# A decoder step's sparse-attention indexer: the new tokens' scores in one step at the head of the chain, with more slack for every index product

## The chip, the cores and the metric

The kernel runs on one core of a Trainium2 chip. The metric is the device time of one execution in microseconds, the median of several runs; lower is better. The core has a matrix engine (PE, with its weight loads shown as PEld), a vector engine (DVE), an activation engine (ACT), a general engine (POOL) and a queue engine (SP) that issues most transfers.

## The reference, cut to what matters

One inference step of one decoder layer: 256 prompt tokens and 64 sample tokens (8 requests of 8 new tokens, each with 2048 cached positions in 16 pages) go through one input projection whose columns feed three head groups; their outputs are gated, joined and go through one output projection and a layer norm. The change touches the indexer of the sample tokens. For each request it scores all 2056 keys, the 2048 cached ones and the 8 new ones, and the top 256 of each query are attended to:

```python
def _indexer_scores(iq, iw, ik):
    dots = jnp.einsum('bthd,bld->bthl', iq.astype(jnp.float32), ik.astype(jnp.float32)) * (D_IDX ** -0.5)
    return jnp.einsum('bth,bthl->btl', iw.astype(jnp.float32) * (H_IDX ** -0.5), jax.nn.relu(dots))
# in _dsa_sample
ik_all = jnp.concatenate([ik_past.astype(ik_new.dtype), ik_new], axis=1)
sc = _indexer_scores(iq, iw, ik_all)
sc = jnp.where(kpos[None, None, :] <= qpos[None, :, None], sc, -jnp.inf)
_, sel = lax.top_k(sc, n_sel)
```

There are 16 index heads of width 64, so a request's 8 queries times 16 heads fill the 128 rows of a product.

## The kernel before, in words

**Data.** Products that need more than one pass of precision are done on split numbers: `ACT.copy` rounds a tile to a short float (`wh` of a weight half `wr`, `xh` of the input), the difference is kept (`wl`, `xl`), and three products stand for one: high by high, low by high, high by low. A weight block of 128 columns by 8 slices of 128 rows comes by one transfer into `wr`; each half of it (512 columns) becomes a pair `wh`, `wl`, ACT making the first and DVE or POOL the second. A half serves 12 products `pj<-x..,w..`, in two quanta of six. There are four buffers each of `wh` and `wl`.

**Order of the work.** One program order is written out by a planner while the kernel is built. `Plan` keeps a reckoned time for each engine and each tile; the main loop at the end of `hymba_step` puts the next piece on PE: a quantum of six projection products, a unit of two cache pages (`KV` or `VACC` products on tiles of 32 columns), or a step of one of the background generators (`bg`). A generator yields `need(tiles, ps=.., lag=..)`, and is taken up again (`met`) when all the tiles are available by the plan for at least `lag` us and `ps` of the buffers `mA`, `mB` in the matrix engine's accumulator memory are free. So a lag is a distance in reckoned time between the operands and the product that reads them: projection quanta are put in between. Once recorded, each engine executes its list in order, and waits where an operand or a buffer is late on the chip.

**The index chain of the sample tokens** is the generator `idx_sample`. It waits for the eight index-query blocks (`iq`), which `ev_iq` adds into the tile `st["q"]` on DVE, and splits that tile: `ACT.copy(qh, q)` and `DVE.tensor_sub(ql, q, qh)`. Then it walks through steps. A step (`stack`) takes 512 keys of each of two requests, stacks high and low parts of the keys above each other (two `ACT.copy` of 64 rows, two `DVE.tensor_sub` of 64 rows), and does four products of 512 columns, two for each request. A relu of each result goes to SBUF on ACT or DVE. After four such pairs of steps `sums` weighs the relus by head and adds them (products on tiles of 32 columns into `va`). Requests come in two halves `sp`; each half had the cached keys in four step pairs and, as the part `c == 2`, the 8 new keys of its four requests in two more steps of four products of 8 columns, with their own sums. That made 20 steps. The cached index keys are gathered by `idx_load` through POOL and SP.

Beside it run `idx_prompt` (index scores of the prompt tokens: blocks of products with 64 rows, into all four `mA`, `mB` buffers, evacuated by ACT into `PT`), and later `topk_sample`, `soft`, the cache pages, `hgrn`, `attn_*`, the memory products and the output projection, which all take their place from the same planner. `LAG2` is the lag of a step's products behind their operands.

Of the kernel before, what the change touches and what calls it, by code (L numbers as in the profile page):

```python
# [38 lines left out]
PATIENCE = 9.0  # L39
SOON = 0.4  # L40
LAG = 1.5
LAG2 = 0.4
VISIT_WAIT = 9.0
HASTE = 2.0
CALM = 4.0
# [175 lines left out]
def need(*aps, ps=1, lag=0.0, visit=0.0):  # L221

    return (aps, ps, lag, visit)
# [3 lines left out]
def hymba_step(ctx: ExitStack, tc: tile.TileContext, I, O):  # L227
# [673 lines left out]
    def idx_sample():  # L901
# [10 lines left out]
        qlr = ql.rearrange("p b h t -> p b (h t)")  # L912
        arena = st["arena"]
        sc = arena[:, 0:HALF]
        steps = [(sp, c, f, a) for sp in range(2) for c in range(3) for f in ((1, 0) if c < 2 else (1,))
                 for a in range(2)]
        more = new([128, 2048], "pg")
        plan.split.add(more.tensor.name)
        st["more"] = 1
        slots = [t[:, 512 * i:512 * i + 512] for t in (early, more) for i in range(4)]  # L920
        small = [early[:, 2784 + 8 * i:2792 + 8 * i] for i in range(8)]
        used = [0, 0]

        def relu_slot(n):
            ring = slots if n > 8 else small
            used[n > 8] += 1
            return ring[used[n > 8] % 8][:, 0:n]

        def sums(sp, rs):

            for c in sorted({c for c, f in rs}):
                n = rs[c, 1][0].shape[-1]
                ps = PS([128, 512], "va") if c < 2 else PS([128, 8])
                for f in (1, 0) if c < 2 else (1,):
                    for g in range(4):
                        PE.matmul(ps[32 * g:32 * g + 32, 0:n], wpad[sp][:, g, f, :], rs[c, f][g],
                                  start=f == 1, stop=f == 0 or c == 2)
                d = sc[:, 512 * c:512 * c + n]
                if sp:
                    DVE.tensor_add(d, d, ps[:, 0:n])  # L940
                elif c < 2:
                    ACT.copy(d, ps[:, 0:n])
                else:
                    DVE.tensor_add(d, ps, tail8)

        def stack(k):

            sp, c, f, a = steps[k]
            if c < 2:
                n, raw = 512, st["ci", 2 * sp + a][:, 1024 * f + 512 * c:1024 * f + 512 * c + 512]  # L950
                kk = [stacked[:, 512 * (2 * (k % 2) + j):512 * (2 * (k % 2) + j) + n] for j in range(2)]
            else:
                n, raw = 8, st["nk", sp][:, 8 * a:8 * a + 8]
                kk = [stacked[:, 2048 + 8 * (4 * sp + 2 * a + j):2056 + 8 * (4 * sp + 2 * a + j)] for j in range(2)]
            for j in range(2):
                own, other = slice(64 * j, 64 * j + 64), slice(64 - 64 * j, 128 - 64 * j)
                ACT.copy(kk[j][own], raw[own])
                DVE.tensor_sub(kk[j][other], raw[own], kk[j][own].bitcast(F32))
            if (c, f) == (1, 0):
                plan.pinned.discard(st["ci", 2 * sp + a].tensor.name)  # L960
                del st["ci", 2 * sp + a]
            return kk

        def keys_in(k):
            if k >= len(steps) or steps[k][1] == 2:
                return True
            sp, c, f, a = steps[k]
            x = st.get(("gathered", 2 * sp + a, c, f))
            return x is not None and all(plan.avail(a) <= plan.now for a in x)

        while not keys_in(0):
            yield
        kk = stack(0)
        rs, full = {}, None
        for k, (sp, c, f, a) in enumerate(steps):
# [6 lines left out]
                PE.matmul(pd[j][:, 0:n], qlr[:, b], kk[j], start=False, stop=True)  # L982
            if full:
                sums(*full)
                full = None
            r = rs.setdefault((c, f), [])
            for j in range(2):
# [2 lines left out]
                    ACT.activation(r[-1], pd[j][:, 0:n], AF.Relu)  # L990
                else:
                    DVE.tensor_scalar(r[-1], pd[j][:, 0:n], 0.0, None, op0=OP.max)
            if a == 1 and (c, f) in ((0, 0), (2, 1)):
                full, rs = (sp, rs), {}
            while not keys_in(k + 1):
                yield
# [1193 lines left out]
```

## Time and profile before

| what | value |
|---|---|
| median of 3 runs | 872.84 us (872.7 to 873.22) |
| the profiled execution | 875.51 us |
| its span, first to last instruction | 873.7 us |
| PE busy | 858.3 us, 98% of the span |
| DVE, ACT, POOL busy | 559.9, 424.2, 307.4 us |
| transfers | 266.51 MB, mean 305 GB/s |
| granted PE clock | 0.997 |

The profiled execution is 2.67 us over the median, and 1.81 us of its time lie outside the span. In rows of the timeline the columns are start, duration (both us), engine, line, operation, tiles written and read, shapes, count, and in brackets the engine's idle time just before with what ended it. All recorded operations have line 155, so tiles tell them apart: `pj` with `xh`, `xl` is a projection product, `cat` is the tile with the stacked keys (`cat_4`) or the relus (`cat_3`), `pg` and `bp` in the index chain are the queries and their split, `PT` receives the prompt's index scores.

### The profile page before, as it was taken

What the parts mean: (1) busy time and instruction counts of PE and PEld (TensorE: products, weight loads), DVE (VectorE), ACT (ScalarE), POOL (GpSimd) and SP (SyncE); (2) the same over time, 40 slices, a digit from 0 to 9 for tenths busy, and PEclk for the clock granted to TensorE, in tenths of its full rate; (3) what the DMA queues carried; (4) which work ended last, traced back from release to release, by engine and by line L of the source; (5) the groups of instructions that cost most, each with busy time, mean ns of one, the idle gap of its engine ahead of it and who ended that gap; (6) DMA issues with size and microseconds to landing.
All of it is one profiled execution on the core that took longest, in us unless ns stands there. A gap on an engine that the chain in (4) does not pass through costs nothing.

```text
span 873.7 us, 19324 instructions
## 1 busy us (share of the span) xinstructions
PE 858.3 (98%) x6974; PEld 730.1 (84%) x6974; DVE 559.9 (64%) x1134; ACT 424.2 (49%) x909; POOL 307.4 (35%) x311
## 2 busy tenths in 40 slices
PE   9999999999999999999999999999999999999996
PEld 8998988888989988878788788777887789888885
DVE  6777989747978983453574476568545235853655
ACT  6434766545445435434454455644454344744432
POOL 0453563255644551141231223334312001533434
PEclk9999999999999999999999999999999999999998
DMA  8654554899999989999989999999999957856633
GB/s 305 189 172 153 158 149 125 292 369 367 394 412 373 374 315 391 371 372 405 387 300 408 409 374 402 365 405 376 344 400 369 410 215 250 310 179 199 195 97 121
DMA packets 84370, 266.51 MB, mean 305 GB/s; under 512 B 10609, under 2 KB 21810, under 8 KB 83634
## 3 DMA queue, kind: packets, MB, share of 16 engines
q1 hardware_dynamic: 83250, 263.18, 81.6%
q0 software_dynamic: 1024, 2.10, 0.8%
q8 instruction: 55, 0.90, 0.4%
q14 instruction: 41, 0.34, 0.1%
HBM read 256.50 MB, written 8.73 MB: 304 GB/s over the span
## 4 chain that ended last, share of the span: by engine, by line
PE 91%; DVE 3%; DMA 2%; ACT 2%; issue 1%; POOL 1%; SPq 0%; DVEq 0%; ACTq 0%; POOLq 0%
PE pj L155 54%; PE mB L155 11%; PE va L155 10%; PE mA L155 8%; PE kv L155 8%; DVE wl L155 1%; DMA wr<-in_wo 1%; ACT wh L155 1%; DMA pg<-in_xT 1%; DVE t L155 1%; DVE pg L155 1%; DMA S<-in_ci,row 0%; ACT t L155 0%; ACT xh L155 0%; POOL S L155 0%
## 5 line engine op out<-in xcount | busy, mean ns | idle before, releaser
L155 ACT CAST wh<-wr 128x512 fp32r<-128x512 f32 x338 | 207.0, 620 | 248.4 <-PE pj L155 189.9
L155 PE MATMUL pj<-xh,wh 128*128 128x320 f32 x1008 | 321.6, 319 | 0.0
L155 PE MATMUL pj<-xh,wl 128*128 128x320 f32 x1008 | 311.6, 309 | 0.3 <-DVE wl L155 0.3
L155 PE MATMUL pj<-xl,wh 128*128 128x320 f32 x1008 | 311.3, 309 | 0.5 <-issue 0.5
L155 DVE TENSOR_TENSOR wl<-wr,wh 128x512 fp32r<-128x512 f32 x237 | 179.2, 766 | 184.6 <-ACT wh L155 177.3
L155 POOL TENSOR_TENSOR wl<-wr,wh 128x512 fp32r<-128x512 f32 x101 | 135.4, 1348 | 283.1 <-ACT wh L155 241.4
L155 PEld LDWEIGHTS pj<-xh,wh 128*128 128x128 f32 x1008 | 189.4, 188 | 17.9 <-issue 14.1
L155 PEld LDWEIGHTS pj<-xl,wh 128*128 128x128 f32 x1008 | 189.5, 188 | 2.0 <-issue 0.7
L155 PEld LDWEIGHTS pj<-xh,wl 128*128 128x128 f32 x1008 | 189.2, 188 | 0.5 <-DVE wl L155 0.5
L155 POOL TENSOR_TENSOR t<-t,t 128x320 f32<-128x320 f32 (+3 forms) x46 | 41.2, 899 | 102.4 <-ACT t L155 55.4
L155 PE MATMUL va<-pg,PT 128*32 128x512 f32 x464 | 58.8, 595 | 0.0
L155 PE MATMUL kv<-pg,qpad 128*32 128x256 f32 (+1 forms) x884 | 57.8, 380 | 0.0
L155 PEld LDWEIGHTS kv<-pg,qpad 128*32 128x32 f32 (+1 forms) x884 | 31.3, 110 | 20.2 <-PE pj L155 1.5
L155 DVE MAX8 PT<-PT 128x8 f32<-128x1032 f32 x32 | 39.5, 1234 | 0.5
L155 DVE MATCH_REPLACE8 PT<-PT 128x1032 f32<-128x1032 f32 x32 | 39.0, 1218 | 0.0
L155 PEld LDWEIGHTS va<-pg,PT 128*32 128x32 f32 x464 | 14.5, 109 | 29.1 <-issue 26.1
L155 POOL DMA_INDIRECT S<-in_ci,row x24 | 27.0, 1125 | 31.2 <-DVE row L155 24.4
L155 POOL TENSOR_TENSOR t<-t,tabm 128x320 f32<-128x320 f32 x16 | 14.1, 878 | 37.5 <-DVE t L155 33.8
L155 ACT ACTIVATE S<-kv 128x512 f32<-128x512 f32 x16 | 9.6, 597 | 30.8 <-PE kv L155 30.8
L155 PE MATMUL mB<-t,wh 128*128 128x256 f32 x128 | 23.7, 283 | 0.0
L155 DVE TENSOR_TENSOR cat<-S,cat 64x512 fp32r<-64x512 f32 x24 | 18.2, 758 | 7.0 <-ACT cat L155 6.2
L155 DVE TENSOR_TENSOR t<-t,t 128x320 f32<-128x320 f32 (+3 forms) x26 | 16.0, 614 | 10.1 <-POOL t L155 5.0
(379 smaller groups left out, 1347.4 us busy)
## 6 DMA issues: line engine op xcount, KB each, us to landing
wr<-in_wt SPq DMA_DIRECT2D x126, 512.0 KB
pg<-in_cv SPq DMA_DIRECT2D x116, 512.0 KB
pg<-in_ck SPq DMA_DIRECT2D x110, 512.0 KB
wr<-in_wo SPq DMA_DIRECT2D x36, 512.0 KB
S<-in_ck SPq DMA_DIRECT2D x18, 512.0 KB
wr<-in_wm SPq DMA_DIRECT2D x16, 512.0 KB
S<-in_cv SPq DMA_DIRECT2D x12, 512.0 KB
pg<-in_cXV SPq DMA_DIRECT2D x8, 512.0 KB
```

The costliest lines, as they stand in the source:

```text
L155: res = f(*a, **k)
```

## The change

The new tokens' part `c == 2` leaves the list of steps, which is now 16 long. A generator `new_tokens` stands ahead of the first step: it stacks the new keys of all eight requests with four copies and four subtractions of 64 rows by 16 columns (before: eight of each, by 8 columns), yields a need with a lag of 2.5 us, passes until the plan is another 1.0 us on, and issues 16 products of 8 columns in one run into one accumulator tile, with one relu over 64 columns (before: four runs of four products, eight relus). `new_sums` weighs all of them in one accumulation of eight products after the first half's sums, with one addition instead of two. `LAG2` goes from 0.4 to 0.8. The number of products is the same.

```diff
-LAG2 = 0.4
+LAG2 = 0.8
@@ idx_sample
-        steps = [(sp, c, f, a) for sp in range(2) for c in range(3) for f in ((1, 0) if c < 2 else (1,))
-                 for a in range(2)]
+        steps = [(sp, c, f, a) for sp in range(2) for c in range(2) for f in (1, 0) for a in range(2)]
...
+        def new_tokens():
+
+            v = stacked[:, 2048:2112].rearrange("p (s a j c) -> p s a j c", s=2, a=2, j=2)
+            for sp in range(2):
+                raw = st["nk", sp].rearrange("p (a c) -> p a c", a=2)
+                for j in range(2):
+                    own, other = slice(64 * j, 64 * j + 64), slice(64 - 64 * j, 128 - 64 * j)
+                    ACT.copy(v[own, sp, :, j], raw[own])
+                    DVE.tensor_sub(v[other, sp, :, j], raw[own], v[own, sp, :, j].bitcast(F32))
+            yield need(ql, qh, v[0:64, 1, :, 1], v[64:128, 1, :, 0], lag=2.5)
+            t = plan.now
+            while plan.now < t + 1.0:
+                yield
+            ps = PS([128, 8, 8])
+            for b in range(8):
+                k = stacked[:, 2048 + 8 * b:2056 + 8 * b]
+                PE.matmul(ps[:, b, :], qh[:, b], k, start=True, stop=False)
+                PE.matmul(ps[:, b, :], qlr[:, b], k, start=False, stop=True)
+            ACT.activation(early[:, 2784:2848], ps.rearrange("p b t -> p (b t)"), AF.Relu)
+
+        def new_sums():
+            r, ps = early[:, 2784:2848], PS([128, 8])
+            for sp in range(2):
+                for g in range(4):
+                    c = 8 * (4 * sp + g)
+                    PE.matmul(ps[32 * g:32 * g + 32, :], wpad[sp][:, g, 1, :], r[:, c:c + 8], start=sp == 0, stop=sp == 1)
+            DVE.tensor_add(sc[:, 1024:HALF], ps, tail8)
...
+        yield from new_tokens()
         while not keys_in(0):
             yield
         kk = stack(0)
...
             if full:
                 sums(*full)
+                if (sp, c) == (0, 1):
+                    new_sums()
                 full = None
...
-            if a == 1 and (c, f) in ((0, 0), (2, 1)):
+            if a == 1 and f == 0:
                 full, rs = (sp, rs), {}
```

The planner's order changes with it from the end of the prompt's last index block on; the first 540 rows of PE's list keep their order up to one quantum. Three places matter below. (In the names, `bp_1152` and `bp_1153` are the high and low part of the queries, `pg_315` the queries, `pg_400` gathered keys, `nk` the new keys.)

**ACT, from the split of the queries on.** Before:

```order
L155 CAST bp_1152<-pg_315 128x1024
L155 CAST cat_4_84<-pg_400 64x512 x2
L155 CAST wh_1167<-wr_1034 128x512
L155 CAST wh_1183<-wr_1034 128x512
L155 CAST wh_1201<-wr_1095 128x512
L155 ACTIVATE PT_512<-mA_1218 128x384
L155 ACTIVATE PT_512<-mA_1219 128x384
```

And now, from the same instruction on:

```order
L155 CAST bp_1152<-pg_315 128x1024
L155 CAST cat_4_84<-nk_72_513 64x2x8 x2
L155 CAST cat_4_84<-nk_73_518 64x2x8 x2
L155 CAST wh_1171<-wr_1034 128x512
L155 CAST wh_1187<-wr_1034 128x512
L155 CAST wh_1212<-wr_1095 128x512
L155 ACTIVATE PT_512<-mA_1219 128x384
```

Two wide copies of gathered keys have given way to four narrow ones of the new keys; the weight halves and the evacuation of the prompt's block follow as before.

**DVE, from the same split on.** Before:

```order
L155 TENSOR_TENSOR pg_315<-t_1142,t_1141 64x8x8 x4
L155 TENSOR_TENSOR bp_1153<-pg_315,bp_1152 128x1024
L155 TENSOR_TENSOR cat_4_84<-pg_400,cat_4_84 64x512 x2
L155 TENSOR_TENSOR wl_1168<-wr_1034,wh_1167 128x512
L155 TENSOR_TENSOR wl_1184<-wr_1034,wh_1183 128x512
```

Now:

```order
L155 TENSOR_TENSOR pg_315<-t_1142,t_1141 64x8x8 x4
L155 TENSOR_TENSOR bp_1153<-pg_315,bp_1152 128x1024
L155 TENSOR_TENSOR cat_4_84<-nk_72_513,cat_4_84 64x2x8 x2
L155 TENSOR_TENSOR cat_4_84<-nk_73_518,cat_4_84 64x2x8 x2
L155 TENSOR_TENSOR wl_1172<-wr_1034,wh_1171 128x512
L155 TENSOR_TENSOR wl_1188<-wr_1034,wh_1187 128x512
```

Everything ahead of these rows on DVE is unchanged, and the first low half of a weight still stands behind the queries' split and the stacked keys.

**PE, after the prompt's last index block.** Before, the block (its last row first), one quantum, the first index product and the next weight half:

```order
L155 MATMUL mB_1221<-t_307,t_1146 128x256
L155 MATMUL pj_1132<-xh,wh_1128 128x320
L155 MATMUL pj_1132<-xl,wh_1128 128x320
L155 MATMUL pj_1132<-xh,wl_1129 128x320
L155 MATMUL pj_1132<-xh,wh_1128 128x320
L155 MATMUL pj_1132<-xl,wh_1128 128x320
L155 MATMUL pj_1132<-xh,wl_1129 128x320
L155 MATMUL mA_1254<-cat_4_84,bp_1152 128x512
L155 MATMUL mA_1254<-cat_4_84,bp_1153 128x512
L155 MATMUL mA_1255<-cat_4_84,bp_1152 128x512
L155 MATMUL mA_1255<-cat_4_84,bp_1153 128x512
L155 MATMUL pj_1276<-xh,wh_1167 128x320
```

Now the block stands one quantum earlier, the two quanta of the half `wh_1128` follow it, and then, with no index product ahead of it, the next half:

```order
L155 MATMUL pj_1132<-xh,wh_1128 128x320
L155 MATMUL pj_1132<-xl,wh_1128 128x320
L155 MATMUL pj_1132<-xh,wl_1129 128x320
L155 MATMUL pj_1261<-xh,wh_1171 128x320
L155 MATMUL pj_1261<-xl,wh_1171 128x320
L155 MATMUL pj_1261<-xh,wl_1172 128x320
```

After 42 projection products behind the block stand the 16 products of 8 columns, after 36 more the first step of 512 columns; later steps have 30 projection products or more between them, most of them 24 before. Further on the same kinds of pieces stand in other neighbourhoods: 45 visits to products on 32 columns between full-width ones (44 before), 64 returns from plain 32-bit products to projection products (59 before). From the transfers of the last input weights on, SP's list is in the same order as before.

More of the change, by code (lines that the diff above doesn't have):

```diff
@@ L920, in idx_sample @@
         slots = [t[:, 512 * i:512 * i + 512] for t in (early, more) for i in range(4)]
-        small = [early[:, 2784 + 8 * i:2792 + 8 * i] for i in range(8)]
-        used = [0, 0]
+        used = [0]
         def relu_slot(n):
-            ring = slots if n > 8 else small
-            used[n > 8] += 1
-            return ring[used[n > 8] % 8][:, 0:n]
+            used[0] += 1
+            return slots[used[0] % 8][:, 0:n]
         def sums(sp, rs):
             for c in sorted({c for c, f in rs}):
-                n = rs[c, 1][0].shape[-1]
-                ps = PS([128, 512], "va") if c < 2 else PS([128, 8])
-                for f in (1, 0) if c < 2 else (1,):
+                ps = PS([128, 512], "va")
+                for f in (1, 0):
@@ L935, in sums @@
                     for g in range(4):
-                        PE.matmul(ps[32 * g:32 * g + 32, 0:n], wpad[sp][:, g, f, :], rs[c, f][g],
-                                  start=f == 1, stop=f == 0 or c == 2)
-                d = sc[:, 512 * c:512 * c + n]
+                        PE.matmul(ps[32 * g:32 * g + 32, :], wpad[sp][:, g, f, :], rs[c, f][g], start=f == 1, stop=f == 0)
+                d = sc[:, 512 * c:512 * c + 512]
                 if sp:
-                    DVE.tensor_add(d, d, ps[:, 0:n])
-                elif c < 2:
-                    ACT.copy(d, ps[:, 0:n])
-                else:
-                    DVE.tensor_add(d, ps, tail8)
+                    DVE.tensor_add(d, d, ps)
+                else:
+                    ACT.copy(d, ps)
@@ L946, in stack @@
+        def new_sums():
[5 more added lines that the diff above has]
+            DVE.tensor_add(sc[:, 1024:HALF], ps, tail8)
         def stack(k):
             sp, c, f, a = steps[k]
[L949 to L954, printed above, removed]
+            raw = st["ci", 2 * sp + a][:, 1024 * f + 512 * c:1024 * f + 512 * c + 512]
+            kk = [stacked[:, 512 * (2 * (k % 2) + j):512 * (2 * (k % 2) + j) + 512] for j in range(2)]
@@ L964, in keys_in @@
         def keys_in(k):
-            if k >= len(steps) or steps[k][1] == 2:
+            if k >= len(steps):
                 return True
```

## The prediction

> **What bounds the kernel now.** First the page: busy times and the chain that ended last.
>
> ```profile
> PE 858.3 (98%) x6974; PEld 730.1 (84%) x6974; DVE 559.9 (64%) x1134; ACT 424.2 (49%) x909; POOL 307.4 (35%) x311
> PE 91%; DVE 3%; DMA 2%; ACT 2%; issue 1%; POOL 1%; SPq 0%; DVEq 0%; ACTq 0%; POOLq 0%
> ```
>
> The matrix engine sets the time from end to end: 91% of the chain is PE at work. So an edit is worth what it takes out of PE's own list, plus the waits in that list that it removes or makes. The second view is who PE waited for, in total over the run (columns: us in total, times, longest).
>
> ```profile
> PE mA L155 <- ACT PT L155: 1.8, 1, 1.8
> ...
> PE mA L155 <- ACT t L155: 1.0, 1, 1.0
> ...
> PE mA L155 <- issue: 0.8, 2, 0.5
> PE mA L155 <- POOL wl L155: 0.7, 1, 0.7
> ```
>
> The longest wait of the run, 1.8 us, is the first index product. The rest is small. The timeline around it, PE first, then ACT, then DVE:
>
> ```profile
> 85.47 0.31 PE L155 MATMUL pj<-xh,wl 128*128 128x320 f32 x1
> 87.55 1.18 PE L155 MATMUL mA<-cat,bp 128*128 128x512 f32 x4 [1.78 <-ACT PT L155]
> 88.57 0.30 PE L155 MATMUL pj<-xh,wh 128*128 128x320 f32 x1
> ...
> 83.22 1.04 ACT L155 CAST bp<-pg 128x1024 fp32r<-128x1024 f32 x1 [6.21 <-DVE pg L155]
> 84.17 1.26 ACT L155 CAST cat<-pg 64x512 fp32r<-64x512 f32 x2
> 85.46 1.66 ACT L155 CAST wh<-wr 128x512 fp32r<-128x512 f32 x3
> 87.02 0.86 ACT L155 ACTIVATE PT<-mA 128x384 f32<-128x384 f32 x2
> ...
> 81.93 0.43 DVE L155 TENSOR_TENSOR t<-t,t 128x256 f32<-128x256 f32 x1 [2.24 <-issue]
> 82.28 0.91 DVE L155 TENSOR_TENSOR pg<-t,t 64x64 f32<-64x64 f32 x4
> 84.30 1.23 DVE L155 TENSOR_TENSOR bp<-pg,bp 128x1024 fp32r<-128x1024 f32 x1 [1.11 <-ACT bp L155]
> 85.56 1.40 DVE L155 TENSOR_TENSOR cat<-pg,cat 64x512 fp32r<-64x512 f32 x2
> 86.99 1.90 DVE L155 TENSOR_TENSOR wl<-wr,wh 128x512 fp32r<-128x512 f32 x3
> ```
>
> The queries are finished on DVE at 83.19 (82.28 + 0.91). ACT stood 6.21 us in front of their split, and behind that one instruction stand the next three weight halves (85.46) and the evacuation of the prompt's block (87.02), whose buffer the index product waits for. On DVE the low half of the queries ends at 85.53, the low keys at 86.96, and only then come the low weight halves. So at 85.6 PE lacks three things at once: the buffer (about 87.4), the stacked keys (86.96), and the next weight half, whose high part starts on ACT at 85.46 and whose low part on DVE at 86.99. The view of waits names only the first.
>
> **The change part by part.**
>
> *The long slack ahead of the first product.* It takes the index product out of the place at 87.55. What stands there then? By the order shown above, the two quanta of the half `wh_1128` behind the prompt's block, and then the half `wh_1171`, the first one cast after the queries' split. All of DVE's list up to that split is unchanged, so the queries come when they came. The price of the new wait, from rows: DVE is free at 85.56; four narrow subtractions of new keys come first. Their nearest rows:
>
> ```profile
> L155 ACT CAST cat<-nk x8: 183/190/197, 125.4 to 184.1; 64x8 fp32r<-64x8 f32 x8
> 128.46 0.35 DVE L155 TENSOR_TENSOR cat<-nk,cat 64x8 fp32r<-64x8 f32 x2
> ```
>
> Four by 0.35 / 2 is 0.7 us, so the first low half starts at 86.3 instead of 86.99. From such a start to the product that reads it:
>
> ```profile
> 76.32 1.28 DVE L155 TENSOR_TENSOR wl<-wr,wh 128x512 fp32r<-128x512 f32 x2
> 77.06 0.41 PE L155 MATMUL pj<-xh,wl 128*128 128x320 f32 x1 [0.26 <-DVE wl L155]
> ```
>
> 0.74 us: PE goes on at about 87.0. When does it run dry? A projection product takes 0.147 us:
>
> ```profile
> 717.45 26.27 PE pj L155 x179
> ```
>
> Before, the last one of the old half began at 85.47, so PE was dry at 85.62 and waited 87.55 - 85.62 = 1.93 us. Now the same work precedes, with the prompt's block one quantum (0.88 us) earlier; the block's last operand is the sum at 81.93 that ends at 82.36, about when the block would now start, which may cost 0.2 us. Two products of the new half read its high part alone: ACT makes four copies of 0.19 us from 84.17, then the cast (the first of 1.66 / 3 us), done by about 85.6. So PE runs to 85.9, or with the 0.2 to 86.1, and waits to 87.0: a loss of 1.1 us either way against 1.93. The subtractions now have 16 columns, not 8, and could take 0.1 us more each. Gain 0.4 to 0.8 us; I take 0.7. The wait does not go away; it passes from the index product to the projection, because what is late is the queries, and the weights queue behind them. The 16 narrow products themselves come 28 projection products later (4.1 us), after 91, when their operands and their buffer have long been there: no wait.
>
> *The doubled slack of the later steps.* One later step of before made PE wait, a narrow one:
>
> ```profile
> 128.03 0.31 PE L155 MATMUL pj<-xh,wl 128*128 128x320 f32 x1
> 128.67 0.61 PE L155 MATMUL mA<-cat,bp 128*128 128x8 f32 x4 [0.33 <-issue]
> ```
>
> 0.64 us from start to start where 0.147 is usual: 0.49 lost, while DVE makes its keys at 128.46. That step is gone, and the remaining ones stand further from their operands: gain 0.49, and no less than 0 if another step takes it over. The 512-column steps show no other wait in the list, so doubling their slack has nothing more to win.
>
> *Sixteen narrow products in one run instead of four runs of four.* One run of before:
>
> ```profile
> 183.08 0.31 PE L155 MATMUL pj<-xh,wl 128*128 128x320 f32 x1
> 183.23 0.50 PE L155 MATMUL mA<-cat,bp 128*128 128x8 f32 x4
> 183.59 0.39 PE L155 MATMUL pj<-xh,wh 128*128 128x320 f32 x1
> 183.82 0.30 PE L155 MATMUL pj<-xl,wh 128*128 128x320 f32 x1
> ```
>
> Four take 0.36 us, and the next projection product has 0.23 instead of 0.147: 0.44 a run, 1.76 for four. Sixteen together take 16 by 0.09 plus one such 0.08, that is 1.5, or up to 1.76 if the first of a run is the cheap one. Gain 0 to 0.3, taken as 0.1. The Trainium skill, TensorE: Matmul & The Clock Gate, section Back-to-back issue gap, would have products of up to 64 columns about 60 cycles of 2.4 GHz apart, 25 ns, while its section LDWEIGHTS (loading the stationary operand) prices the load of 128 columns at 107 ns; by the first alone the run would cost 0.4 us and the gain be 1.3 us, but the 90 ns in the rows above agree with the second, so it is not counted. The relus, copies and subtractions saved are on ACT and DVE, which here are 49% and 64% busy; their one effect on PE is the 0.7 us in the first term.
>
> *What the new order adds.* A visit to the 32-column tiles of a cache unit, and a block of plain 32-bit products, each cost PE a turn:
>
> ```profile
> 195.51 0.31 PE L155 MATMUL pj<-xh,wl 128*128 128x320 f32 x1
> 195.75 1.93 PE L155 MATMUL kv<-S,qpad 128*32 128x256 f32 x32
> 197.50 1.91 PE L155 MATMUL kv<-pg,qpad 128*32 128x256 f32 x32
> 199.34 0.41 PE L155 MATMUL pj<-xh,wh 128*128 128x320 f32 x1
> 199.59 0.30 PE L155 MATMUL pj<-xl,wh 128*128 128x320 f32 x1
> ...
> 206.40 0.50 PE L155 MATMUL pj<-xh,wh 128*128 128x320 f32 x1
> 206.73 0.31 PE L155 MATMUL pj<-xl,wh 128*128 128x320 f32 x1
> ```
>
> Into the visit 0.24 instead of 0.147; its second 32 products take 1.84 against 1.75 for the first, the rest being the way out; then 0.25 instead of 0.147: together 0.09 + 0.09 + 0.10 = 0.28 us, once more than before. After a block of 32-bit products the second projection product starts 0.33 after the first, 0.19 too late; five more returns cost up to 0.95, and nothing if the handover ahead of them is shorter by as much. I take 0.4.
>
> *Sum.* -0.7 - 0.49 - 0.1 + 0.28 + 0.4 = -0.6 us: 875.51 becomes 874.9 in a profiled execution, and, the profile standing 2.67 over the median, 872.84 becomes 872.2. With every bound at its good end the terms give -0.8 - 0.49 - 0.3 + 0.28 + 0 = -1.3 (871.5), at the bad end -0.4 - 0 - 0 + 0.28 + 0.95 = +0.8 (873.7). The end of the program should not move: SP's list is the same there, and PE's last straight run of projection products still separates the last cache unit from the output projection.
>
> **The rivals.**
>
> *The wait's removal is worth all of it, and the later stages lose waits too* (faster). If the low weight half were on time, 1.93 + 0.49 would be gained instead of 1.2 (0.7 + 0.49). Against it: DVE cannot begin that half before 85.53, since the queries' low half stands ahead. For it: behind the index phase every piece has a new neighbour, and the wait on `t` (1.0 us) and the waits named issue, both between soft products and their evacuations, may fall away. Half of 1.0 + 0.8 + 0.7 on top of the full 2.4, less the 0.7 of turns, is -2.95, 869.9; by the sum with those waits alone gone, -0.6 - 1.8 = -2.4, 870.4. About 870.2.
>
> *The memory products meet the mask products* (slower). The list now puts the last requests' mask products one at a time between quanta of the memory projection, which holds both `pj` and both `mB` buffers; before, they stood ahead of it with both pairs to use. With two `mA` buffers left, each of the four wide ones can find its buffer still read by DVE:
>
> ```profile
> 547.62 0.69 DVE L155 CUSTOM_DVE_ANT_0 S<-S,mA 128x512 f32<-128x512 f32 x1 [3.19 <-PE mA L155]
> ```
>
> Four by 0.69 is 2.8 us; with the sum -0.6 that is +2.2, 875.0. It decides once DVE is a whole such pass behind at that place. Against it: by the plan a buffer is asked for only when it is free, and up to 18 memory products stand between two mask products.
>
> *The change does not do what it says*: its slack is reckoned time, and the queries are late on the chip by more than the plan knows. Then the narrow run waits itself. Ruled out as far as the rows go: it stands 4 us behind the late queries. Without any of its gains the turns alone give +0.7, 873.5, still no change.
>
> **How the numbers follow.** Chances: my sum 0.53, faster rival 0.28, slower rival 0.16, the last 0.03. A measurement of this kernel tells about 0.2% from no change, 1.75 us: faster is below 871.1, slower above 874.6. My sum and the last lie within; the faster rival is nearly all below, the slower nearly all above. So faster 0.28, same 0.55, slower 0.17. Predicted 872.2, its own range 871.2 to 873.7, the bounds of the sum and the spread of the runs shown; the range for 8 in 10 takes in most of both rivals: 869.7 to 875.1.
>
> **What would show it.** Right: PE's longest wait near 86 to 87 us is still there, about 1 us, but stands before a `pj` product and is put down to `wl`; the narrow run, after 91 us, has no idle time; ACT's idle time before the split of the queries is still 6 us. Wrong: no wait there at all, or one at the narrow run; or a PE list whose waits between 200 and 700 us differ by more than 2 us in sum from before, which would say that the reshuffle decides and not the slack.

## The result, and the profile after

The changed kernel takes 868.36 us (median of 5 runs, 867.72 to 868.72) where the kernel before takes 873.01 (5 runs, 872.7 to 873.22): a ratio of 0.9946, 95% interval 0.9935 to 0.9957, 4.65 us faster. The prediction said 872.2, in a range of 869.7 to 875.1.

The page of the changed kernel, busy times and chain (the profiled execution took 868.29 us, its span 866.5):

```profile
PE 856.6 (99%) x6972; PEld 729.7 (84%) x6974; DVE 555.4 (64%) x1133; ACT 422.7 (49%) x900; POOL 299.1 (35%) x305
PE 97%; DVE 1%; DMA 1%; SPq 0%; issue 0%; ACT 0%; DVEq 0%
```

PE does the same products (two of them have no record here), but the chain is now 97% PE where it was 91%. The view of whom PE waited for shows what went (us in total, times, longest):

```profile
PE kv L1881 <- DVE t L155: 1.1, 1, 1.1
PE mB L155 <- DVE t L155: 0.3, 1, 0.3
PE va L155 <- DVE xl L155: 0.2, 1, 0.2
PE pj L155 <- DVE pg L155: 0.2, 1, 0.2
```

The 1.1 us at the top is in the program's first microseconds, and before had it too. All four waits that the prediction quoted are gone: 1.8 on `PT`, 1.0 on `t`, 0.8 on issue and 0.7 on `wl`. Two of them lie near 650 and 760 us, far from any index product.

The place of the first index product, in the timeline of the changed kernel, PE, then ACT, DVE and POOL:

```profile
85.52 0.31 PE L155 MATMUL pj<-xl,wh 128*128 128x320 f32 x1
85.66 0.33 PE L155 MATMUL pj<-xh,wl 128*128 128x320 f32 x1
...
89.64 0.31 PE L155 MATMUL pj<-xh,wl 128*128 128x320 f32 x1
89.79 1.84 PE L155 MATMUL mA<-cat,bp 128*128 128x8 f32 x16
91.49 0.39 PE L155 MATMUL pj<-xh,wh 128*128 128x320 f32 x1
91.72 0.31 PE L155 MATMUL pj<-xl,wh 128*128 128x320 f32 x1
...
81.69 1.05 ACT L155 CAST bp<-pg 128x1024 fp32r<-128x1024 f32 x1 [4.39 <-DVE pg L155]
...
82.77 1.23 DVE L155 TENSOR_TENSOR bp<-pg,bp 128x1024 fp32r<-128x1024 f32 x1 [1.11 <-ACT bp L155]
84.03 0.77 DVE L155 TENSOR_TENSOR cat<-nk,cat 64x16 fp32r<-64x16 f32 x4
84.83 1.29 DVE L155 TENSOR_TENSOR wl<-wr,wh 128x512 fp32r<-128x512 f32 x2
...
77.03 1.18 POOL L155 DMA_INDIRECT S<-in_ci,row  x1 [4.27 <-DVE row L155]
```

No product waits there. The product at 85.66 is the first to read the new low half; the prediction had about 1.1 us of waiting before it. The split of the queries begins at 81.69, not at 83.22, and ACT stood 4.39 us before it, not 6.21, although nothing on DVE or POOL ahead of it had been edited. The gather of cached keys on POOL took 1.18 us here. In the first profile of before it took longer:

```profile
77.96 1.78 POOL L155 DMA_INDIRECT S<-in_ci,row  x1 [4.26 <-DVE row L155]
```

This leaves three questions: did the wait pass to the projection or not; was the first profile of before an unusual execution; and where do the 2 to 3 us come from that lie nowhere near the index chain?

### The profile page after: what moved, and what is told of

The parts are those of the page before. It is cut to its first block, busy times and chain, and to the rows that moved or that the text cites. A ratio compares the mean times of both kernels' runs of the same rounds, so it can differ in the third digit from the quotient of the medians.

```text
span 866.5 us, 19303 instructions
## 1 busy us (share of the span) xinstructions
PE 856.6 (99%) x6972; PEld 729.7 (84%) x6974; DVE 555.4 (64%) x1133; ACT 422.7 (49%) x900; POOL 299.1 (35%) x305
## 4 chain that ended last, share of the span: by engine, by line
PE 97%; DVE 1%; DMA 1%; SPq 0%; issue 0%; ACT 0%; DVEq 0%
PE pj L155 57%; PE mB L155 12%; PE va L155 10%; PE mA L155 10%; PE kv L155 8%; DMA pg<-in_xT 1%; DVE pg L155 0%; DVE t L155 0%; DVE s L155 0%; SPq L155 0%; DVE xl L155 0%; ACT xh L155 0%; DVE wl L155 0%; DVEq L2196 0%; DVE bns L155 0%
## 5 line engine op out<-in xcount | busy, mean ns | idle before, releaser
L155 ACT CAST wh<-wr 128x512 fp32r<-128x512 f32 x338 | 207.4, 619 | 255.7 <-PE pj L155 203.4
L155 PE MATMUL pj<-xh,wh 128*128 128x320 f32 x1008 | 322.0, 319 | 0.0
L155 PE MATMUL pj<-xh,wl 128*128 128x320 f32 x1008 | 311.5, 309 | 0.0
L155 PE MATMUL pj<-xl,wh 128*128 128x320 f32 x1008 | 311.3, 309 | 0.0
L155 DVE TENSOR_TENSOR wl<-wr,wh 128x512 fp32r<-128x512 f32 x239 | 181.9, 770 | 190.8 <-ACT wh L155 183.3
L155 POOL TENSOR_TENSOR wl<-wr,wh 128x512 fp32r<-128x512 f32 x99 | 131.8, 1335 | 235.4 <-ACT wh L155 217.9
L155 PEld LDWEIGHTS pj<-xh,wh 128*128 128x128 f32 x1008 | 189.4, 188 | 18.2 <-issue 13.5
L155 PEld LDWEIGHTS pj<-xl,wh 128*128 128x128 f32 x1008 | 189.5, 188 | 1.4
L155 PEld LDWEIGHTS pj<-xh,wl 128*128 128x128 f32 x1008 | 189.2, 188 | 0.0
L155 POOL TENSOR_TENSOR t<-t,t 128x320 f32<-128x320 f32 (+3 forms) x44 | 39.5, 898 | 129.6 <-ACT t L155 68.2
L155 PE MATMUL kv<-pg,qpad 128*32 128x256 f32 (+1 forms) x916 | 59.2, 380 | 0.0
L155 PE MATMUL va<-pg,PT 128*32 128x512 f32 x456 | 58.5, 595 | 0.0
L155 PEld LDWEIGHTS kv<-pg,qpad 128*32 128x32 f32 (+1 forms) x916 | 31.5, 110 | 21.1 <-issue 1.9
L155 DVE MAX8 PT<-PT 128x8 f32<-128x1032 f32 x32 | 39.5, 1233 | 0.5
L155 DVE MATCH_REPLACE8 PT<-PT 128x1032 f32<-128x1032 f32 x32 | 39.0, 1218 | 0.0
L155 PEld LDWEIGHTS va<-pg,PT 128*32 128x32 f32 x456 | 14.6, 109 | 29.0 <-issue 26.3
L155 POOL DMA_INDIRECT S<-in_ci,row x24 | 26.0, 1084 | 31.6 <-DVE row L155 22.0
L155 POOL TENSOR_TENSOR t<-t,tabm 128x320 f32<-128x320 f32 x16 | 14.1, 879 | 34.2 <-DVE t L155 32.6
L155 PE MATMUL mB<-t,wh 128*128 128x256 f32 x128 | 24.5, 290 | 0.0
L155 POOL TENSOR_TENSOR xl<-cat,xh 128x256 fp32r<-128x256 f32 x12 | 13.4, 1142 | 27.2 <-ACT xh L155 27.2
L155 POOL TENSOR_TENSOR bp<-t,bp 128x128 f32<-128x128 f32 (+1 forms) x17 | 10.4, 615 | 35.4 <-ACT bp L155 35.3
L155 ACT ACTIVATE S<-kv 128x512 f32<-128x512 f32 x16 | 9.5, 596 | 26.4 <-PE kv L155 23.2
```

Of the source, the lines that this page charges most:

```text
L155: res = f(*a, **k)
```

## The experiments

Kernels measured together from here on shared a chip and the runs of before beside them, so ratios are compared, not times of different sets. Times are medians; brackets hold 95% intervals. "Head" is the stretch around the first index product, "the order behind" is PE's order after the index phase; a "draw" is one such order as the planner happens to write it. In kernels with a longer recording helper its lines show as L160 and L165 instead of L155.

### The kernel before, a second time

No edit. 

> The kernel before, unchanged, profiled a second time. Three theories of where 4.65 us went. Passed-on wait (the prediction): the queries come at 83.2 us in every execution, so the split of the queries starts on ACT at 83.2 again, PE waits 1.9 us before the first index product, and the gathers on POOL just ahead take 2.39 us (near 60.5) and 1.78 us (near 78) as in the first profile. Chance: the first profile, 2.67 us over the median, had late queries; then a second profile shows a split at 81.7 to 82.2 (as the changed kernel does, 81.69), gathers of 1.78 and 1.18 us, and a wait of 0.4 to 0.9 us. Neighbours: whatever the head does, the waits on t, wl and the ident product between 400 and 760 us (0.63, 0.66, 0.68, 1.16, 0.84 us in the first profile) stand again within 0.2 us each, because they follow from the order. Time: 873.0 +- 0.3, ratio 1.000.

873.97 us against 874.71, ratio 0.9993 [0.9983, 1.0003].

```profile
77.16 1.78 POOL L155 DMA_INDIRECT S<-in_ci,row  x1 [4.26 <-DVE row L155]
82.43 1.04 ACT L155 CAST bp<-pg 128x1024 fp32r<-128x1024 f32 x1 [5.39 <-DVE pg L155]
86.76 1.20 PE L155 MATMUL mA<-cat,bp 128*128 128x512 f32 x4 [1.49 <-ACT PT L155]
...
647.88 1.13 PE L155 MATMUL mA<-t,t 128*128 128x256 f32 x4 [0.99 <-ACT t L155]
```

The queries come 0.8 us earlier than in the first profile, at neither of the two times that had been expected (83.2, or 81.7 to 82.2), and the wait at the head is 1.65 us (start to start, against the usual 0.147) instead of 1.94. The stalls further on stand where they stood: 0.69 us before the `ident` product near 618, 1.15 near 648, 0.63 near 402. Two are missing, 0.84 us near 760 and 0.43 near 77; across the profiles of kernels with this order the first of them measures between nothing and 0.84, so it goes with the execution. This one takes 873.24 us, 2.27 less than the first profile.

### The first index products alone, 12 projection products later

An edit in the recorded order: the calls of the first step are kept and made 12 `pj` products later, while the planner reckons as if they had been made. (The lines that keep the calls and make them later are left out here.)

```diff
+            if k == 0:
+                plan.later = []
             for j in range(2):
                 b = 4 * sp + 2 * a + j
                 PE.matmul(pd[j][:, 0:n], qh[:, b], kk[j], start=True, stop=False)
...
+            if k == 0:
+                plan.due, plan.later = [12, plan.later], None
```

> The kernel before with one edit in the recorded order: the four first index products (and their two relus) are handed over 12 projection products later; every other instruction of PE, DVE, POOL and SP keeps its place, ACT's list differs in the place of the two relus. Passed-on wait (the prediction): about 1.1 us of the 1.93 is found again before the first projection product that reads the new low half, gain 0.7 us, 872.3. Whole wait: nothing waits there, gain 1.9 us, 871.1. Chance (the queries are earlier in usual executions): the wait was only 0.4 to 0.9 in the timed runs, gain 0.4 to 0.9, with no wait before the projection.

874.45 against 874.71, ratio 0.9998 [0.9988, 1.0009]: no change that can be measured. A gain of 0.4 us, or the 0.7 that the prediction expected, would lie inside that interval; the whole wait of 1.9 us would not.

```profile
86.92 0.42 PE L160 MATMUL pj<-xh,wl 128*128 128x320 f32 x1 [1.05 <-DVE wl L160]
```

The wait passes on, as predicted: 1.22 us too late from start to start, before the first product that reads the new low half, and put down to `wl`. Against 1.65 in the other profile from that chip 0.43 us are left as gain in the profile, less than the 0.7 of the first theory; the whole wait was not to be had.

### The long slack alone, on the first step of before

```diff
-            yield need(ql, qh, *kk, ps=2, lag=LAG2)
+            yield need(ql, qh, *kk, ps=2, lag=2.5 if k == 0 else LAG2)
+            t = plan.now
+            while k == 0 and plan.now < t + 1.0:
+                yield
```

> The kernel before with the long slack (2.5 us, then another 1.0) before its first index step, and nothing else: the step leaves 42 projection products later, and the later index steps close up behind it, so that from the second part of the program on the order on PE is that of before (the list differs in 134 rows, all between the first and the ninth step). Passed-on wait: gain 0.7, 872.3. Whole wait: 1.9, 871.1. Neighbours: the waits between 400 and 760 us stand as before, so the time cannot come below 870.9 (1.9 and at most 0.2 more); if it comes near 868.4, the long slack explains the whole of the change by itself.

875.18 against 874.71, ratio 1.0005 [0.9995, 1.0015].

```profile
85.96 0.41 PE L155 MATMUL pj<-xh,wh 128*128 128x320 f32 x1 [0.28 <-ACT wh L155]
87.57 0.41 PE L155 MATMUL pj<-xh,wl 128*128 128x320 f32 x1 [1.05 <-DVE wl L155]
```

The projection waits twice, 0.45 and 1.21 us, as much in sum as the index product had waited. Behind it the steps stand closer, and the index phase loses about 1 us more than before. A slack by itself, with the weights still queued behind the queries and the wide keys, gains nothing.

### The later steps alone, one quantum later

The same device for the third to the nineteenth step, by 6 products: `k == 0` becomes `2 <= k < len(steps) - 1`, and 12 becomes 6; the sums keep their place. 

> The kernel before with one edit in the recorded order: the products of the third to the nineteenth index step (and their relus) are handed over one quantum, six projection products, later, which is about what the doubled slack does; the order of everything else on PE and DVE is kept, POOL's and SP's lists are identical. Direct slack: if the slack itself carries the 4 us that it brought alone, they appear here too, ratio 0.995. Neighbours: only the index phase gains, its 0.5 us before the narrow step and some 0.15 us inside wide steps, 0.5 to 1.1 us in all, ratio 0.9987 to 0.9994; the waits near 618 (0.69) and 648 us (1.15), which the doubled slack alone had lost, stand in the profile.

871.54 against 872.64, ratio 0.9989 [0.9980, 0.9998].

```profile
85.93 1.20 PE L160 MATMUL mA<-cat,bp 128*128 128x512 f32 x4 [0.51 <-ACT PT L160]
...
127.02 0.31 PE L160 MATMUL pj<-xh,wl 128*128 128x320 f32 x1
127.16 0.50 PE L165 MATMUL mA<-cat,bp 128*128 128x8 f32 x4
...
645.34 1.13 PE L160 MATMUL mA<-t,t 128*128 128x256 f32 x4 [0.99 <-ACT t L160]
```

The narrow step follows its projection product after 0.14 us; its 0.49 is gone, and so are delays of 0.11 to 0.15 us inside wide steps. The stall at 645 (648 before) stands. So the slack's own worth is 1.1 us (by the interval 0.2 to 1.7). On this chip the gather took 1.18 us (76.94), the queries were split at 81.60, and the wait at the head of the old order is only 0.68 us.

### One stall far from the index chain

The kernel above, and the score product of one prompt head before which PE stood at 645, with its two DVE readers, six projection products later:

```diff
         ps = PS([128, 2, 256])
+        if h == 1:
+            plan.later = []
         for tt in range(2):
             PE.matmul(ps[:, tt, :], MQ[h][:, 128 * tt:128 * tt + 128], st["mkT"][h], start=True, stop=True)
...
+        if h == 1:
+            plan.due, plan.later = [6, plan.later], None
```

> The kernel of the third to nineteenth step handed over one quantum later, with a second edit in the recorded order: one score product of a prompt head in the memory part, the one before which PE waits 1.15 us (0.99 of them for an ACT copy) near 645, is handed over six projection products (0.88 us) later with its two DVE readers; ACT's, DVE's, POOL's and SP's lists are unchanged. Neighbours: a stall far from the index chain is worth its length, 0.9 us more than the first edit alone, ratio to before 0.9979. Hidden anyway: another wait takes its place within the same stage, ratio 0.9989 as the first edit alone.

870.85 against 872.87, ratio 0.9977 [0.9968, 0.9986].

```profile
645.36 1.13 PE L165 MATMUL mA<-t,t 128*128 128x256 f32 x4
651.20 0.72 PE L160 MATMUL mB<-ident,t 128*128 128x128 f32 x4 [0.30 <-DVE t L160]
```

The wait at 645 falls from 1.15 to 0.28 us, a new one of 0.47 appears before 651.20, so 0.4 us are left as gain in the profile. The ratio is 0.0012 lower than that of the first edit alone, about 1 us, but the two come from different sets and their intervals overlap. This fits a stall far from the index chain being worth its length; it does not show it.

### The doubled slack alone, and other slacks

```diff
-LAG2 = 0.4
+LAG2 = 0.8
```

> The kernel before with the slack of the later steps doubled (0.4 to 0.8) and nothing else. The first two steps stand where they stood; from the third step on the order differs. The sum of the prediction: the narrow step's 0.49 us goes, the 1.9 us at the head stay, 872.5. Neighbours: the order behind differs in over 2000 rows, so the waits between 400 and 760 us are drawn anew; they lose up to 4 us or gain as much, 869 to 876, and the head still shows its wait before the first index product. If the time is 868.4 with the head's wait in place, the doubled slack carries the gain and the new-token step is idle.

870.49 against 874.71, ratio 0.9954 [0.9939, 0.9968]: nearly the whole gain of the change, with the head's wait still there (1.59 us). The kernel before took 874.71 us on that chip, more than the 873.01 of the first set, so this was measured again beside the changed kernel:

> The doubled slack alone once more, beside the changed kernel on one chip. If the first measurement (0.9954) holds: ratio to before 0.994 to 0.9965, and within 0.001 of the changed kernel's. If the slower chip made it look better: 0.9965 to 0.998, as the lost time in its profile (2 us less than before's second profile, and 1 us less of turns) would give.

869.23 against 873.03, ratio 0.9956 [0.9943, 0.9969]. It holds. Now the same line with 0.6, 1.0 and 1.2:

> The kernel before with the later steps' slack at 0.6, half of the way. Between the steps stand 30 projection products, the same as with 0.8, so the index phase loses 0.2 us here as there. Direct slack: then the time is that of 0.8, ratio 0.9954 +- 0.001. Neighbours: the order behind the index phase differs from both (3700 rows against before), the waits between 400 and 760 us are drawn anew, and the ratio may lie anywhere from 0.994 to 1.001; the difference from 0.8 equals that of PE's lost time outside the index phase in the two profiles.

> The kernel before with the later steps' slack at 1.0, between 0.8 (0.9954 so far) and 1.2 (0.9981). Direct slack: between the two. Neighbours: anywhere from 0.994 to 1.003.

> The kernel before with the later steps' slack at 1.2, three times. The index phase again has 30 or more projection products between steps; the first step leaves one quantum later. Direct slack: no slower than 0.8, ratio at most 0.9954 +- 0.001. Neighbours: anywhere from 0.994 to 1.001, and not ordered by the slack; the head still waits 1 to 1.6 us, before the index product or before a projection.

| slack of the later steps, rest as before | ratio to before |
|---|---|
| 0.4 (before, again) | 0.9993 [0.9983, 1.0003] |
| 0.6 | 1.0030 [1.0018, 1.0041] |
| 0.8 | 0.9954 [0.9939, 0.9968] and 0.9956 [0.9943, 0.9969] |
| 1.0 | 0.9946 [0.9934, 0.9958] |
| 1.2 | 0.9981 [0.9971, 0.9990] |

The time does not follow the slack. At 0.6 the later steps have the same 30 products between them as at 0.8, and the kernel is slower than before, and slower than either expectation had it; there PE waited for a cache page, near 549 us:

```profile
PE kv L155 <- DMA S<-in_ck: 2.6, 1, 2.6
```

Right behind this wait the granted clock is 0.50 (551 to 553 us) where it was 1.00, for 3.4 us in all, and what runs there takes about twice as long. That is some 1.7 us more, an estimate from half of the 3.4, so wait and spell together cost about 4.3 us in this profile. Of the twelve runs the two with a mean granted clock of 0.998 took 872.69 and 873.28 us, the two with 0.994 took 877.42 and 877.47; runs of before beside them at 0.998 took 872.29 to 873.96. The first two are level with before, although the slack's own 1.1 us are in them; whether what they lack is this wait, no profile shows.

At 1.2 one narrow step of the index phase waits 0.98 us at 139, and PE waits 0.95 us for a cache page at 246.

### The new tokens' step without the doubled slack, and without the long slack

```diff
-LAG2 = 0.8
+LAG2 = 0.4
```

> The changed kernel with the slack of the later steps put back to 0.4: the new tokens' step with its long slack alone. Direct slack: the gain hangs on the doubled slack, so most of it is lost, ratio to the kernel before 0.998 to 1.0. Head: the narrow run leaves 42 projection products behind the prompt's block as in the changed kernel and no wait stands near 86 us, so 1.2 to 1.7 us are gained there, ratio 0.998. Neighbours: the order behind the head is drawn anew (it differs from the changed kernel's in 2600 rows), so the sum of the waits between 400 and 760 us may lie anywhere between the changed kernel's and 4 us more: ratio 0.994 to 1.000.

869.95 against 872.64, ratio 0.9966 [0.9954, 0.9979]. And the changed kernel without its long slack:

```diff
-            yield need(ql, qh, v[0:64, 1, :, 1], v[64:128, 1, :, 0], lag=2.5)
-            t = plan.now
-            while plan.now < t + 1.0:
-                yield
+            yield need(ql, qh, v[0:64, 1, :, 1], v[64:128, 1, :, 0], lag=LAG2)
```

> The changed kernel without the long slack ahead of the new tokens' products: the 16 narrow products stand six projection products behind the prompt's last block, where before had its first index product. Passed-on wait: they wait for the low half of the queries, 1 to 1.6 us near 86, and the time is 1 to 1.6 us over the changed kernel, ratio to before 0.996 to 0.998, if the order behind costs the same. Chance of neighbours: that order differs in 2800 rows and may add or take some 2 us.

870.25 against 872.64, ratio 0.9975 [0.9965, 0.9984], 2.2 us over the changed kernel in the same set.

```profile
85.44 1.95 PE L155 MATMUL mA<-cat,bp 128*128 128x8 f32 x16 [0.99 <-ACT PT L155]
```

Here the narrow run waits, 1.0 us. The rest of the 2.2 is not so clear: seven of the twelve runs, at a granted clock of 0.998, have a median of 869.95, 1.9 us over the changed kernel, and the five at 0.993 to 0.997 took 870.90 to 872.72. No profile shows what lowered the clock in these. The parts do not add up: 0.8 alone brings 3.8 us, the step alone 2.7, both together 4.6.

### The changed kernel again

> The changed kernel, unchanged, profiled a second time. In its first profile the gather on POOL near 77 us took 1.18 us where the five profiles of kernels with the old head have 1.78, the split of the queries began at 81.69 us and no product waited near 86. Chance: the gather may take 1.78 us here; then the split begins at 82.4 and a wait of 0.1 to 0.7 us stands before the first projection product that reads a new low half. Order: if it is 1.18 again, the shorter gather belongs to the order of the changed kernel. Time: 0.9946 +- 0.001 of the kernel before.

868.06 against 872.64, ratio 0.9946 [0.9934, 0.9959]; gather 1.18 us, no wait near 86. Once more beside the doubled slack alone:

> The changed kernel once more, beside the doubled slack alone: ratio to before 0.9946 +- 0.001 as twice before; PE waits for nothing longer than 0.6 us between 60 and 700 us.

868.03 against 873.03, ratio 0.9941 [0.9928, 0.9953]. With a slack of 1.2, and of 1.0, for the later steps:

> The changed kernel with the later steps' slack at 1.2 instead of 0.8; the head up to the narrow run is the same, the order behind differs in 1150 rows. Direct slack: the same time as the changed kernel or less, ratio to before 0.9946 or lower. Neighbours: the same head without a wait, and the sum of the waits behind 145 us between 1 us less and 3 us more than in the changed kernel: ratio 0.9935 to 0.998.

869.32 against 872.87, ratio 0.9962 [0.9949, 0.9974].

> The changed kernel with the later steps' slack at 1.0 instead of 0.8; PE's order differs in 26 rows, one index step one quantum later. Both theories: the same time as the changed kernel within 0.001, 0.9943; a larger difference would say that the measurement tells less than its interval claims.

869.76 against 874.69, ratio 0.9955 [0.9940, 0.9969]. On this last chip the gather near 77 took 1.78 us with the new head too, and then the wait that the prediction had named is there:

```profile
86.39 0.42 PE L155 MATMUL pj<-xh,wl 128*128 128x320 f32 x1 [0.79 <-DVE wl L155]
```

### Only the order behind is drawn anew

One number that has nothing to do with the index chain: how long a visit to products on 32-column tiles is put off. First in the kernel before, whose order is unchanged to about 240 us:

```diff
-VISIT_WAIT = 9.0
+VISIT_WAIT = 11.0
```

> The kernel before with one unrelated planner number changed: the patience with which a visit to products on 32-column tiles is put off (11 instead of 9 reckoned us). Head and index phase are the same row by row; the order on PE differs from about 240 us on, in 2300 rows. Neighbours: the time moves by 1 us or more in either direction (ratio under 0.9988 or over 1.0012), the waits near 618 and 648 us vanish or others come, while the waits near 86 and 128 us stand. Common cause in the index edits: ratio 1.000 within 0.0012.

870.36 against 873.03, ratio 0.9965 [0.9953, 0.9977]. The waits of head and index phase are those of before:

```profile
85.77 1.19 PE L155 MATMUL mA<-cat,bp 128*128 128x512 f32 x4 [0.48 <-ACT PT L155]
126.88 0.61 PE L155 MATMUL mA<-cat,bp 128*128 128x8 f32 x4 [0.33 <-DVE cat L155]
```

2.7 us are gained, and no index product was moved. Then the same line in the changed kernel:

> The changed kernel with the unrelated planner number (visits put off 11 instead of 9 reckoned us): head and index phase as in the changed kernel, the order behind differs in 756 rows. Neighbours: another draw, ratio to before between 0.993 and 0.998; the changed kernel's lost time behind 350 us is already low (4.9 us against before's 6.8), so a slower result is likelier than a faster one. If the changed kernel's gain behind the index chain came from the edit itself, 0.9943 +- 0.001 again.

874.58 against 874.69, ratio 1.0000 [0.9990, 1.0010], outside the 0.993 to 0.998 that were expected of a new draw: with the whole change in place, nothing is gained. The changed kernel with a slack of 1.0, whose order on PE differs from the changed one in 26 rows, has 869.76 beside it.

```profile
86.60 0.41 PE L155 MATMUL pj<-xh,wl 128*128 128x320 f32 x1 [0.73 <-DVE wl L155]
...
612.50 0.31 PE L155 MATMUL pj<-xh,wl 128*128 128x320 f32 x1
616.13 0.55 PE L155 MATMUL mB<-ident,t 128*128 128x128 f32 x3 [3.33 <-ACT t L155]
...
617.14 0.47 PE L155 MATMUL pj<-xh,wh 128*128 128x320 f32 x1
617.40 0.47 PE L155 MATMUL pj<-xl,wh 128*128 128x320 f32 x1
```

Three transpositions of `hgrn` ask for a buffer of `mB` that by the profile an ACT copy still reads, and PE stands 3.3 us; the copy itself begins only at 615.71, after 2.42 us in which ACT waited for DVE. Behind it the projection products come 0.26 to 0.27 us apart where 0.147 is usual, until 620.1; the granted clock from 618 to 620 us is 0.50. That is some 1.6 us more (3.82 us from 616.43 to 620.25 for 15 products that usually take 2.2). This one wait and what follows it take the 4.8 us between the two kernels. The first row shows the long gather again.

### The time that PE loses, by stage

For each profile: the distance from the start of one product to the next, less the usual distance (30th percentile over twelve profiles) of the same two kinds of products, where more than 0.1 us is over; rows inside the 32-column visits and the returns from 32-bit products are left out. Over all twenty profiles, with slightly other exclusions, the sums come out 1.2 to 1.6 lower and their differences change by at most 0.4. In us:

| kernel | head 60 to 95 | index 95 to 210 | 210 to 545 | 545 to 610 | 610 to 700 | from 700 | sum |
|---|---|---|---|---|---|---|---|
| before, first profile | 4.0 | 1.8 | 3.3 | 0.9 | 2.9 | 1.5 | 14.3 |
| before, second | 3.2 | 1.8 | 3.4 | 1.2 | 3.0 | 0.1 | 12.7 |
| later steps one quantum later | 2.2 | 0.7 | 3.0 | 0.9 | 2.9 | 1.0 | 10.8 |
| doubled slack alone, again | 2.2 | 0.6 | 4.1 | 1.3 | 1.0 | 0.2 | 9.5 |
| before, order behind redrawn | 2.2 | 1.8 | 2.6 | 2.0 | 0.9 | 0.4 | 9.8 |
| changed | 1.4 | 0.7 | 2.9 | 1.5 | 1.6 | 0.5 | 8.7 |
| changed, order behind redrawn | 2.4 | 0.6 | 2.8 | 1.6 | 5.8 | 0.5 | 13.7 |

The head's column differs by about 1.0 us with the chip (short or long gather). The stage from 610 to 700 loses 2.5 to 3.0 us wherever the old order behind was kept, and 0.8 to 1.6 in the redrawn orders, except 2.4 with the slack of 1.0 in before and 5.8 in the last row, the stall at 616 with its spell of half clock.

## Why the prediction was wrong, point by point

**What bounds the kernel** was read rightly: PE's own list and the stalls in it. The profiles' spans went with the stalls found in PE's list and with the sequence of its products, and in two of them with the half clock behind the longest stalls.

**The long slack** was priced at 0.7 us, and 0.7 is what it brings with the narrow keys, read from the stalls (no run times it alone): with the short gather the old head waits 0.68 us and the new one not at all; with the long gather the old head waits 1.65 (in the second profile of before) and the new one 0.89 to 0.95. The mechanism was right too, and what the prediction offered as its proof is there when the queries are late: a wait before a `pj` product, put down to `wl`, of 0.73 and 0.79 us of idle time with the new head. What failed is "the queries come when they came": the split of the queries began anywhere from 81.2 to 83.2 us. The prediction took 83.2 from one execution that was 2.67 us over the median, and knew that. So two of its own signs are missing in the first profile of the changed kernel: there is no wait near 86 us, and ACT's idle time before the split is 4.39 us, not 6.

**The doubled slack** was priced at 0.49, with "nothing more to win" in the wide steps. The narrow step's 0.49 went as said. The index phase lost 1.1 us less in all, since products inside two wide steps had also come 0.11 to 0.15 us late, two in each; only waits ahead of a step had been looked for. A term half the size it should have had.

**The narrow run** was priced at a gain of 0.1. The 16 products take 91.49 - 89.79 = 1.70 us and the next projection product 0.08 more, 1.78 against 1.76 for four runs of four: nothing gained. That is 106 ns each. In the Trainium skill, TensorE: Matmul & The Clock Gate, section LDWEIGHTS (loading the stationary operand), the formula comes to 107 ns for a load of 128 columns, which is an estimate, and the section Back-to-back issue gap has a floor of 25 ns. The trace agrees with the first and not with the second, though the runs of four before, at 90 ns a product, lie below the first. In the profile each of these loads lasts 187 to 192 ns, but they overlap; that the loads set the pace is not tested here.

**What the new order adds** is the step that failed. It was taken as turns alone, +0.68 us, with all waits behind the index chain left where they were. Visits did go from 44 to 45, but of the dear returns from 32-bit products two were added (0.19 each), not five. What is left of 4.65 after 1.1 and 0.7 is 2.8 us, a gain where a loss of 0.68 was forecast. The stalls behind the index phase are about 1.2 us shorter than in the second profile of before (7.7 to 6.5 by the table). The rest does not stand in stalls: priced at the usual distances the sequence of products became 1.1 to 1.6 us cheaper, but only 0.2 to 0.8 where the kinds of products are told apart by the tiles that they write and read, so the size of this part rests on the pricing. That the order is worth this much is shown by runs: with the head's wait left in place the doubled slack brought 3.8 us, and about the same slack with the order kept brought 1.1, which leaves 2.7 for the order; redrawn alone, without any change to the index chain, the order brought 2.7 (these are differences of medians, each good to about 1 us); and redrawn in the changed kernel it cost as much as the whole change had won, with the index phase's loss still at 0.6.

**The end of the program** did not move, as predicted: between PE's last product and the end lie 8.0 us in the profiles of before and of the changed kernel.

**The rivals.** The faster one named the right place, "the later stages lose waits too", and was priced at 870.2, since only half of three named waits was counted. It should have been no rival but the main term, with both signs: draws of the order behind ran from -3.4 us (slack 1.0, less its own 1.1) to a loss (slack 0.6; the changed kernel redrawn, 4.8 us behind the changed kernel with a slack of 1.0). The slower rival, memory products against mask products, is not seen: nothing in the view of waits names it. And the test that the prediction set itself, stalls between 200 and 700 us more than 2 us apart, would have missed: they differ by 1.6 from the second profile of before.

What stays open: why a projection product near 400 us comes 0.6 to 1.25 us late in several kernels (the profile says issue), and which neighbours make the sequence of the changed kernel cheaper, and by how much; no run separates it.

## What to carry to other kernels

Where a planner writes the order, an edit to one slack is two edits: the local one, which can be read from the stalls at its place, and a new draw of everything behind it, which here was worth more than the local one and may take either sign. Measure the two apart: move the instructions in the recorded order with the plan left alone for the first, and change an unrelated number for the second. And a wait that is taken away is gained only as far as the next work in line has its own operands; look up what is queued behind the late one on the engine that feeds it.

## What the runs showed of the hardware

The same gather on POOL near 77 us took 1.18 or 1.78 us, and the one near 60 took 1.78 or, once, 2.39: steps of 0.6. All kernels measured on one chip agreed (1.78 in four kernels on one chip and in two on another, 1.18 in twelve on three others), with the old order and the new; for the first profiles, 1.78 in before and 1.18 in the changed kernel, the chip is not on record. The delay reaches the queries through an addition on POOL that DVE waits for, here with the long gather (the second profile of before) and with the short one (the later steps alone):

```profile
81.14 0.43 DVE L155 TENSOR_TENSOR t<-t,t 128x256 f32<-128x256 f32 x1 [2.24 <-POOL t L155]
80.31 0.43 DVE L160 TENSOR_TENSOR t<-t,t 128x256 f32<-128x256 f32 x1 [1.59 <-POOL t L160]
```

PE's stall at the head goes with it, by 0.9 to 1.0 us: before the first index product of the old order it is 1.59 to 1.65 us against 0.63 to 0.69 (1.94 where both gathers were long), and with the new order 0.89 to 0.95 against none.

The clock fell to half behind the two longest stalls. In eighteen of the twenty profiles PE is never idle for more than 1.8 us between 20 us and its last product, and from 11 us on the granted clock is 0.5 only behind that last product. In the two others, after 2.62 us of idle time (slack 0.6, near 549) and after 3.33 (the changed kernel redrawn, near 616), it is 0.5 for 3.4 us, beginning 0.6 us after PE resumed. So a stall of that length cost some 1.6 us beyond itself here. No profile has an idle time between 1.8 and 2.6 us, so none shows from what length on this happens.

The mean granted clock, 0.997 or 0.998 in most runs, was 0.993 to 0.996 in some, and the time was longer with it: 4.7 us between 0.998 and 0.994 for one and the same kernel. In the two profiles at 0.995 and 0.996 the low mean comes with the spell at half clock, and so from a stall in the order itself; for the runs without a profile the cause is not shown.
